# Hybrid trunk, layer 0's attention heads: later value products and joins, earlier raw weight loads, output weights on GpSimd's queue

## The chip, the cores and the metric

The kernel runs on one core of a Trainium2 chip. The time is device microseconds of one execution. Three executions before the change took 2606.33, 2608.89 and 2603.97 us (median 2606.33); a fourth was profiled.

A core has five instruction streams. PE is TensorE (its weight loads are told apart as PEld), DVE is VectorE, ACT is ScalarE, POOL is GpSimd and SP is SyncE. Each works through its own list in order and stops where an instruction waits for another engine or a transfer. Transfers are issued by SP's list or by POOL's, on two different queues, and are carried by the same 16 DMA engines.

## The reference

One sequence of 1024 rows of width 1024 goes through two layers: a token mixer, a residual add and a squared-ReLU MLP each. Layer 0's mixer is what the change touches:

```python
def dilated_attention(h, w_in, w_out):
    qkv = (h @ w_in).reshape(B, S, N_GROUPS, 3, ATTN_HEADS, HEAD_DIM)
    cos, sin = rope_tables(S, HEAD_DIM)
    for g, (window, dil) in enumerate(((128, 1), (512, 4), (2048, 16))):
        q = apply_rope(qkv[:, :, g, 0], cos, sin) * (HEAD_DIM ** -0.5)
        k = apply_rope(qkv[:, :, g, 1], cos, sin)
        v = qkv[:, :, g, 2]
        o_g, lse_g = dilated_group_attention(q, k, v, dil, window // dil)
        ...
    alpha = jax.nn.softmax(jnp.stack(lses, axis=0), axis=0)
    o = jnp.sum(alpha[..., None] * jnp.stack(outs, axis=0), axis=0)
    return o.reshape(B, S, ATTN_WIDTH).astype(h.dtype) @ w_out
```

There are 8 heads of width 128, and each head attends in three groups (dilations 1, 4, 16). The three outputs of a head are merged with weights from their softmax denominators. Everything is float32; the kernel multiplies matrices as three products of split operands (high by high, high by low, low by high).

## The kernel before

The values of all groups come first (lines with `pA` and `pB`). Then 24 steps follow, one per head and group: step p has head p // 3 and group p % 3. A step multiplies the normed input by the query and key weights of its group, in seven products of a Strassen-like scheme, in the order `SLOTS = (0, 1, 3, 2, 6, 4, 5)`. Each product is split in two halves of six matmuls (128x128 by 128x512). So a step has 14 half products, and these are its clock.

All other work of the heads is hung on this clock. `at(t, fn, rank)` puts a piece of work on an agenda, and `advance()`, which is called behind every half product, runs what is due, in the order of the ranks. With c = 14 p for the step that runs, the pieces are:

- `column` (L1121 to L1145), four times a step at c+5, c+11, c+13, c+15: DVE adds two products into a half of q or k (L1127), SP swaps its halves by two transfers (L1128 and L1129, `cw<-c`), and four half products later DVE turns it with the rotary tables and writes `qT` or `kT` (L1136, L1137 and L1139 or L1144). The last of these, half of `qT`, falls on c+5 of the next step.
- `follow`: the attention of the step before. It has four pairs of row blocks. `scores` (PE, L989) at c+8, c+8, c+12, c+12, then `soft` (DVE L1003, ACT L1005), then `halves` at c+11, c+12, c+15, c+16 (ACT L1035 splits the weights into 16-bit halves, POOL writes them to `pscr`, L1037), then `flip` at c+14, c+15, c+18, c+19 (SP reads them back transposed, L1048, `pt<-pscr`), then `values` at c+20, c+20, c+24, c+24 (PE multiplies them by v, L1069, `pO`; behind the second and the fourth pair ACT copies the result and SP stores it into `og`). c+20 is c+6 of the step behind. The last two steps' attention uses transposes on PE instead.
- `load`: the raw weights of the step behind, four transfers of 256 KB (L1119). `stage` splits them on ACT (L536) and DVE (L537).
- `plan_merges`: when a head's three groups are done, in the steps of group 1 and after. For each half of the rows SP loads 780 KB of `rows` (L1207), DVE makes the weights (`merge_weights` L1214 and L1215, `merge_shares` L1220 to L1223), ACT scales (L1227) and DVE joins (`merge_join` L1231 and L1232); SP stores the join into `oscr`.

```python
POINTS = (8, 8, 12, 12), (11, 12, 15, 16), (20, 20, 24, 24), (14, 15, 18, 19)   # scores, halves, values, flips
...
for s in self.SLOTS:
    for half in range(2):
        self.product(p, s, range(2 * half, 2 * half + 2))
        advance()
```

In the last step (p = 23) the output projection's first weights are fetched as well: `W.dma` (L136, 512 KB each) twice at c+1 and twice at c+2, at rank 0, and at c+3 `ahead_h8` (L1292), which loads 1 MB of joined heads (`ol`). `turned.turn` transposes `ol` on PE at c+8 (L260).

Tiles named k4 share 25 buffers and t2 tiles share 8; a tile takes over a buffer when what used it is done, and the instruction that first writes it waits for that. There are eight PSUM banks. A transfer also waits until the transfer issued eight places before it on its list has landed.

Of the kernel before, what the change touches and what calls it, by code (L numbers as in the profile page):

```python
# [20 lines left out]
P = 128  # L21
# [21 lines left out]
def hybrid_trunk(ctx, tc, x, norm_mix, norm_mlp, norm_fin, a_in, a_out, g_in, g_up, g_b, g_nw,  # L43
                 g_out, m_up, m_down, tab, msk, gmask, ident_d, out):
    nc = tc.nc
    pe, act, dve, pool, sp = nc.tensor, nc.scalar, nc.vector, nc.gpsimd, nc.sync
# [7 lines left out]
    def h8(shape, dt, name):  # L54
        return wk.tile(shape, dt, name=name, tag="h8", bufs=12)

    def k4(shape, dt, name):
        return wk.tile(shape, dt, name=name, tag="k4", bufs=25)

    def t2(shape, dt, name):  # L60
        return wk.tile(shape, dt, name=name, tag="t2", bufs=8)
# [50 lines left out]
    class Weights:  # L112
# [14 lines left out]
            self.slots.append(src)  # L127
            self.by.append(by)

        def dma(self):  # L130
            n = self.ndma
            if n < len(self.slots):
                self.ndma += 1
                src = self.slots[n]
                self.raws[n] = k4([P] + list(src.shape[1:]), F32, "raw")
                sp.dma_start(self.raws[n], src)  # L136

        def prep(self, eng=dve):
            n = self.nprep
# [41 lines left out]
    W = Weights()  # L181
# [104 lines left out]
    class Split:  # L286
# [4 lines left out]
        @staticmethod  # L291
        def at(tiles, k):
            n = 4 // len(tiles)
            return tiles[k // n][:, k % n, :]
# [442 lines left out]
    oscr = drp.tile([S, D], F32, name="oscr")  # L737
# [241 lines left out]
    class Attention:  # L979
# [104 lines left out]
        def plan(self, c, points, turn, values, flip=None):  # L1084
            self.by_dma = flip is not None

            def get():
                self.v = load_values(self.g, self.h)
            at(c + points[0] - 2, get)
            for j in range(4):  # L1090
                t = c + points[j]
                at(t, lambda j=j: self.scores(j), 2)
                at(t + 1 + (j % 2 and points[j] == points[j - 1]), lambda j=j: self.soft(j), 2)
                if self.by_dma:
                    at(c + turn[j], lambda j=j: self.halves(j), 3)
                    at(c + flip[j], lambda j=j: self.flip(j), 3)
                else:
                    at(c + turn[j], lambda j=j: self.turn(j), 3)
                at(c + values[j], lambda j=j: self.values(j), 4)

    class Heads(Up):
# [54 lines left out]
        def plan(self, p):  # L1156
            c = 14 * p
            st = self.st.setdefault(p, {})
            self.behind = True

            def keep(b, name):
                def fn():
                    e = t2([P, 512], F32, name)
                    act.activation(e, st[b], AF.Copy)
                    st[name] = e
                return fn
            at(c + 3, keep("X", "e1"), 0)
            at(c + 5, lambda: self.column(p, 0, 0, st["Y"], st["e1"]), 1)
            at(c + 7, keep("V", "e5"), 0)
            at(c + 9, keep("X", "e2"), 0)  # L1170
            at(c + 11, lambda: self.column(p, 1, 0, st["V"], st["e2"]), 1)
            at(c + 13, keep("X", "e3"), 0)
            at(c + 13, lambda: self.column(p, 1, 1, st["X"], st["e5"]), 1)
            at(c + 15, lambda: self.column(p, 0, 1, st["Z"], st["e3"]), 1)
            if p == 0:
                for s, t in ((4, 1), (6, 3), (5, 5)):
                    at(c + t, lambda s=s: self.stage(p, s), 7)
            at(c + 3, lambda: self.load(p + 1))
            for s, t in ((0, 8), (1, 9), (2, 10), (3, 11), (4, 14), (6, 15), (5, 17)):
                at(c + t, lambda s=s: self.stage(p + 1, s), 7)  # L1180

        def run_head(self, p):
            self.plan(p)
            if p:
                self.follow(p - 1, 14 * p, self.POINTS if p < self.count - 1 else self.SINGLE)
            for s in self.SLOTS:
# [1 line left out]
                    self.product(p, s, range(2 * half, 2 * half + 2))  # L1188
                    advance()

        POINTS = (8, 8, 12, 12), (11, 12, 15, 16), (20, 20, 24, 24), (14, 15, 18, 19)
        SINGLE = (8, 10, 12, 14), (12, 14, 16, 18), (14, 16, 18, 20)

        def follow(self, p, c, points):
# [8 lines left out]
    def merge_load(h, half):  # L1203

        rows = (h8([P, 4, NG, HD + 2], F32, "rows") if h == HEADS - 1 and half else
                r6([P, 4, NG, HD + 2], "rows"))
        sp.dma_start(rows, og[h][512 * half:512 * half + 512].rearrange("(t p) g c -> p t g c", p=P))  # L1207
        return rows
# [71 lines left out]
    def merged(h, half, o):  # L1280
        if h < HEADS - 1:
            sp.dma_start(oscr[512 * half:512 * half + 512, HD * h:HD * h + HD].rearrange("(b p) c -> p b c", p=P), o)
        else:
            def last():
                t_head(h, half, o)
                reached.add((0, half))
            at(clock[0] + 7, last)

    def ahead_h8(pairs):

        t = h8([P, 4, 512], F32, "ol")
        sp.dma_start(t, oscr[512 * pairs:512 * pairs + 512, 0:512].rearrange("(b p) c -> p b c", p=P))  # L1292
        return [t[:, 0:2, :], t[:, 2:4, :]]

    def ahead_k4(p):
# [4 lines left out]
    def plan_merges(h, c):  # L1300

        rows, part = {}, {}

        def load(half):
            rows[half] = merge_load(h, half)

        def weigh(half):
            part[half] = merge_weights(rows[half])

        def join(half):  # L1310
            del part[half]
            merged(h, half, merge_join(rows.pop(half), dve))
        for half in range(2):
            t = c + 13 + 11 * half
            at(t, lambda half=half: load(half))
            if half and h == HEADS - 2:
                t += 9
            at(t + 4, lambda half=half: weigh(half), 9)
            at(t + 5, lambda half=half: merge_shares(rows[half], *part[half]), 9)
            for n in range(4):  # L1320
                at(t + 6 + n, lambda half=half, n=n: merge_scale(rows[half], part[half][1], n), 9)
            at(t + 10, lambda half=half: join(half), 9)
# [429 lines left out]
    ol = []  # L1752
    turned = Turned(ol, x[0])
    for p in range(heads.count):
        h, g = divmod(p, NG)
        if g == 1 and h:
            plan_merges(h - 1, 14 * p)
        if p == heads.count - 1:
            for k in range(0, KT, 2):
                add_rows(a_out, k)  # L1760
            c = 14 * p
            at(c + 1, lambda: (W.dma(), W.dma()), 0)
            at(c + 2, lambda: (W.dma(), W.dma()), 0)
            at(c + 3, lambda: ol.extend(ahead_h8(0)), 0)
            for t in (5, 6, 7, 8):
                at(c + t, lambda: W.prep(dve), 7)
            at(c + 8, lambda: turned.turn(0), 7)
            at(c + 9, lambda: (turned.load_x(0), turned.load_x(1)))
            at(c + 11, lambda: turned.turn(1), 7)
            at(c + 17, lambda: ol.extend(ahead_h8(1)), 9)  # L1770
        heads.run_head(p)
# [619 lines left out]
    ol, turn1 = [], []  # L2391
# [81 lines left out]
```

## Time and profile before

| | us |
|---|---|
| median of three executions | 2606.33 |
| the profiled execution | 2608.73 |
| its span | 2607.0 |
| PE busy | 2569.7 (99%) |
| DVE busy | 1865.2 (72%) |
| ACT busy | 1309.1 (50%) |
| granted TensorE clock, mean | 0.996 |

The span runs from the first to the last instruction that the profile shows; the profiled execution took 1.7 us more. PE's idle time is the difference of its busy time and the span, 37 us. The views of waits name, for each instruction that found its engine idle, what ended the wait. In rows of the timeline the first number is the start in us from the span's start, the second the duration, and a bracket gives the idle time ahead and what ended it.

The 24 steps with their attention lie between about 265 and 890 us.

### The profile page before, as it was taken

The page shows a single profiled execution, that of the slowest core. Times are in us where ns is not written, and L with a number is a line of the kernel's source. Part 1 is how long each engine was busy: PE and PEld are TensorE (multiplying, and loading weights), DVE is VectorE, ACT ScalarE, POOL GpSimd, SP SyncE. Part 2 cuts the span into 40 slices and gives each one's busy share as a digit, 9 for nine tenths or more (in the row PEclk, how much of TensorE's full clock was granted, in tenths as well). Part 3 has the DMA queues.
Part 4 walks back from the last instruction along what each step waited for, and adds up shares of the span by engine and source line. Part 5 has one row for each costly group of instructions (what it writes and reads, how often), then busy time and mean ns, then how long its engine had stood idle before and what let it go on. Part 6 is the DMA issues. An engine that isn't in the chain of part 4 may idle for free.

```text
span 2607.0 us, 33382 instructions
## 1 busy us (share of the span) xinstructions
PE 2569.7 (99%) x11901; PEld 2138.2 (82%) x11901; DVE 1865.2 (72%) x3018; ACT 1309.1 (50%) x2388; POOL 79.3 (3%) x132
## 2 busy tenths in 40 slices
PE   9999999999998999999999999999999999999998
PEld 7888888888787888888888888888888888888887
DVE  7745888888887668766657487887658866656567
ACT  6423566666665446555534345654426555553334
POOL 0000111111110000000000000000000000000000
PEclk9999999999999999999999999999999999999999
DMA  5543688788888732544775453463513544396543
GB/s 182 172 143 109 171 210 213 203 208 216 207 212 219 238 121 100 191 153 154 257 268 185 145 184 106 124 213 99 183 67 127 170 150 161 126 354 205 182 149 131
DMA packets 403705, 456.73 MB, mean 175 GB/s; under 512 B 92337, under 2 KB 264753, under 8 KB 403538
## 3 DMA queue, kind: packets, MB, share of 16 engines
q1 hardware_dynamic: 397250, 437.29, 55.3%
q0 software_dynamic: 6144, 17.05, 2.1%
q8 instruction: 93, 1.52, 0.2%
q14 instruction: 74, 0.61, 0.1%
q10 hardware_dynamic: 144, 0.26, 0.0%
HBM read 279.19 MB, written 133.10 MB: 158 GB/s over the span
## 4 chain that ended last, share of the span: by engine, by line
PE 87%; DMA 5%; DVE 4%; ACT 2%; SPq 1%; issue 1%; DVEq 0%; ACTq 0%
PE pX L599 15%; PE pB L1936 13%; PE pA L1936 10%; PE pV L599 9%; PE pB L830 8%; PE pA L830 5%; PE pY L599 5%; PE pZ L599 5%; PE pd L216 3%; PE pd L214 3%; PE pd L215 3%; DMA cw<-c 2%; DMA pt<-pscr 1%; PE pS L989 1%; PE pO L1069 1%
## 5 line engine op out<-in xcount | busy, mean ns | idle before, releaser
L1936 PE MATMUL pB<-dh 128*128 128x512 f32 x512 | 199.4, 389 | 0.0
L1936 PE MATMUL pB<-dh,dl 128*128 128x512 f32 x512 | 199.2, 389 | 0.0
L1936 PE MATMUL pB<-dl,dh 128*128 128x512 f32 x512 | 199.2, 389 | 0.0
L223 DVE TENSOR_TENSOR dl<-sin,dh 128x1024 fp32r<-128x1024 f32 x112 | 136.7, 1220 | 42.1 <-ACT dh L220 41.4
L220 ACT ACTIVATE dh<-sin 128x1024 fp32r<-128x1024 f32 x112 | 117.9, 1052 | 88.6 <-PE pB L1936 34.1
L220 ACT ACTIVATE dh<-kept 128x1024 fp32r<-128x1024 f32 x64 | 67.9, 1061 | 183.4 <-DVE kept L1901 138.1
L599 PE MATMUL pV<-s4h,wd 128*128 128x512 f32 x448 | 150.9, 399 | 0.0
L1936 PE MATMUL pA<-dh 128*128 128x512 f32 x384 | 149.4, 389 | 0.0
L1936 PE MATMUL pA<-dl,dh 128*128 128x512 f32 x384 | 149.4, 389 | 0.0
L1936 PE MATMUL pA<-dh,dl 128*128 128x512 f32 x384 | 149.4, 389 | 0.0
L1005 ACT ACTIVATE pt<-pt,orow 128x128 f32<-128x128 f32 (+1 forms) x192 | 84.7, 442 | 123.7 <-DVE orow L1003 122.5
L1936 PEld LDWEIGHTS pB<-dh 128*128 128x128 f32 x512 | 96.1, 188 | 20.0
L1936 PEld LDWEIGHTS pB<-dh,dl 128*128 128x128 f32 x512 | 96.1, 188 | 19.9
L1936 PEld LDWEIGHTS pB<-dl,dh 128*128 128x128 f32 x512 | 96.1, 188 | 19.9
L537 DVE TENSOR_TENSOR wal<-raw,wah 128x512 fp32r<-128x512 f32 x112 | 76.2, 686 | 41.1 <-ACT wah L536 41.1
L1069 PE MATMUL pO<-v,pt 128*128 128x128 f32 x560 | 79.2, 284 | 23.1 <-DMA pt<-pscr 22.7
L537 DVE TENSOR_TENSOR wbl<-t,wbh 128x1024 fp32r<-128x1024 f32 x56 | 68.6, 1225 | 46.3 <-ACT wbh L536 46.2
L608 ACT ACTIVATE c<-c 128x512 f32<-128x512 f32 x64 | 40.4, 631 | 118.6 <-DVE c L636 77.6
L1037 POOL DMA_DIRECT2D pscr<-pt x124 | 77.0, 621 | 752.3 <-ACT pt L1035 742.0
L1069 PEld LDWEIGHTS pO<-v,pt 128*128 128x128 f32 x560 | 73.5, 195 | 31.3 <-DMA pt<-pscr 27.7
L599 PEld LDWEIGHTS pV<-s4h,wd 128*128 128x128 f32 x448 | 84.2, 188 | 17.8 <-DVE rb L624 0.3
L223 DVE TENSOR_TENSOR dl<-kept,dh 128x1024 fp32r<-128x1024 f32 x64 | 78.4, 1225 | 24.7 <-ACT dh L220 18.7
(398 smaller groups left out, 7444.3 us busy)
## 6 DMA issues: line engine op xcount, KB each, us to landing
sin<-acts SPq DMA_DIRECT2D x112, 512.0 KB, 3.9
raw<-in_mlp_w_up_dram SPq DMA_DIRECT2D x64, 512.0 KB, 6.2
acts<-s SPq DMA_DIRECT2D x64, 512.0 KB, 3.3
raw<-in_mlp_w_down_dram SPq DMA_DIRECT2D x64, 512.0 KB, 4.7
raw<-in_attn_w_in_dram SPq DMA_DIRECT2D x98, 256.0 KB, 4.5
cw<-c SPq DMA_DIRECT2D x192, 128.0 KB, 3.2
acts<-c SPq DMA_DIRECT2D x64, 256.0 KB, 2.1
kept<-in_mlp_w_down_dram SPq DMA_DIRECT2D x32, 512.0 KB, 5.2
```

Of the source, the lines that this page charges most:

```text
L214: pe.matmul(ps, sh, mh, start=start, stop=False)
L215: pe.matmul(ps, sh, ml, start=False, stop=False)
L216: pe.matmul(ps, sl, mh, start=False, stop=stop)
L220: act.activation(hi, src, AF.Copy)
L223: dve.tensor_tensor(lo, src, hi.bitcast(F32), op=OP.subtract)
L537: self.remain(lambda: dve.tensor_tensor(lo, src, hi.bitcast(F32), op=OP.subtract))
L599: pe.matmul(st[b], u[:, k, :], v, start=first and k + n == 0, stop=k == 3 and n == 2, skip_group_check=True)
L830: pe.matmul(self.acc[s][t], a[:, c], b[:, k, :], start=fresh and m + k + v == 0, stop=m == 1 and k == 1 and v == 2, skip_group_check=True)
L1005: act.activation(pt[:, i, :128 * n], pt[:, i, :128 * n], AF.Exp, scale=-1.0, bias=m, accum_out=self.row[:, r, HD:HD + 1])
L1037: pool.dma_start(scr[512 * P * b:][:256 * P * nb * m].rearrange("(i p c) -> p i c", i=nb, p=P), part.rearrange("p (i c) -> p i c", i=nb))
L1069: pe.matmul(po[:, 2 * (j % 2) + i, :], self.turned(j, tile_, i, s), self.v[:, k0 // 128 + s, :], start=(s == 0), stop=(s == nk - 1))
L1936: pe.matmul(self.acc[s][t], a[:, k, c], b[:, k, :], start=fresh and m + k + v == 0, stop=m == 7 and k == 1 and v == 2, skip_group_check=True)
```

## The change

The raw weights' `load` moves from c+3 to c+1. The value products move from c+20 and c+24 to c+21 and c+25. All of `plan_merges` moves one half product later: the load of the rows from c+13 and c+24 to c+14 and c+25, weights, shares, scaling and joins with it (of head 6's second half only the load moves; the work behind it stays where it was). In the last step `W.dma` and the first `ahead_h8` are issued by POOL instead of SP.

```diff
-        def dma(self):
+        def dma(self, by=None):
...
-                sp.dma_start(self.raws[n], src)
+                (by or sp).dma_start(self.raws[n], src)
...
-            at(c + 3, lambda: self.load(p + 1))
+            at(c + 1, lambda: self.load(p + 1))
...
-        POINTS = (8, 8, 12, 12), (11, 12, 15, 16), (20, 20, 24, 24), (14, 15, 18, 19)
+        POINTS = (8, 8, 12, 12), (11, 12, 15, 16), (21, 21, 25, 25), (14, 15, 18, 19)
...
-    def ahead_h8(pairs):
+    def ahead_h8(pairs, by=sp):
...
-        sp.dma_start(t, oscr[512 * pairs:512 * pairs + 512, 0:512].rearrange("(b p) c -> p b c", p=P))
+        by.dma_start(t, oscr[512 * pairs:512 * pairs + 512, 0:512].rearrange("(b p) c -> p b c", p=P))
...
         for half in range(2):
-            t = c + 13 + 11 * half
+            t = c + 14 + 11 * half
             at(t, lambda half=half: load(half))
             if half and h == HEADS - 2:
-                t += 9
+                t += 8
             at(t + 4, lambda half=half: weigh(half), 9)
             at(t + 5, lambda half=half: merge_shares(rows[half], *part[half]), 9)
             for n in range(4):
                 at(t + 6 + n, lambda half=half, n=n: merge_scale(rows[half], part[half][1], n), 9)
             at(t + 10, lambda half=half: join(half), 9)
...
-            at(c + 1, lambda: (W.dma(), W.dma()), 0)
-            at(c + 2, lambda: (W.dma(), W.dma()), 0)
-            at(c + 3, lambda: ol.extend(ahead_h8(0)), 0)
+            at(c + 1, lambda: (W.dma(pool), W.dma(pool)), 0)
+            at(c + 2, lambda: (W.dma(pool), W.dma(pool)), 0)
+            at(c + 3, lambda: ol.extend(ahead_h8(0, pool)), 0)
```

On PE the first pair's and second pair's value products (`pO`) stand behind the first half of the product `pX<-s2`, where before they stood ahead of it:

```order
+L599 MATMUL pX<-s2l,wbh 128x512
+L599 MATMUL pX<-s2h,wbl 128x512
 L1069 MATMUL pO<-v,pt 128x128 x7
-L599 MATMUL pX<-s2h,wbh 128x512
-L599 MATMUL pX<-s2l,wbh 128x512
```

Six matmuls pass the products at c+6, and six others (`pX<-s3`) in the same way at c+10.

On SP, in the step of group 1, this is the stretch from the end of one step's stores to the next step's first flips (`og_70` is head 0's output, `rows` the merge's load):

```order
-L1207 DMA rows<-og_70 128x4x390
+L1082 DMA og_70<-orow 128x4x130
+L1128 DMA cw<-c 64x512
+L1129 DMA cw<-c 64x512
 L1048 DMA_TRANSPOSE pt<-pscr_96 128x1x256
 L1048 DMA_TRANSPOSE pt<-pscr_96 128x2x256
+L1207 DMA rows<-og_70 128x4x390
 L1128 DMA cw<-c 64x512
 L1129 DMA cw<-c 64x512
```

The load of the rows goes behind the first pair's flips, and the last store of `og` behind a pair of swaps. The four loads of raw weights (L1119) are in no such piece: they stand behind the second pair's flips and ahead of the third's in both kernels. They take other k4 buffers.

On DVE, in the step of group 2, the last rotary work on `qT` (L1136, L1137, L1144) passes the shares of the merge (L1220 to L1223):

```order
+L1127 TENSOR_TENSOR c<-pY,e_3043 128x512
+L1136 TENSOR_TENSOR cw<-cw,tab 128x512
+L1137 TENSOR_TENSOR c<-c,tab 128x512
+L1144 TENSOR_TENSOR qT<-c,cw 128x4x128
 L1220 TENSOR_TENSOR md<-me,rows 128x12
 L1221 TENSOR_REDUCE mz<-md 128x4
 L1222 RECIPROCAL mz<-mz 128x4
 L1223 TENSOR_TENSOR me<-me,mz 128x12
-L1127 TENSOR_TENSOR c<-pY,e_3037 128x512
```

POOL's list in the last step, where only writes of weights' halves stood:

```order
 L1037 DMA pscr_97<-pt 128x2x512
+L136 DMA raw<-in_attn_w_out_dram 128x1024 x2
 L1037 DMA pscr_98<-pt 128x2x512
+L136 DMA raw<-in_attn_w_out_dram 128x1024 x2
 L1037 DMA pscr_99<-pt 128x2x512
+L1292 DMA ol<-oscr 128x4x512
```

The third pair's write (`pscr_98`) now stands behind two weight loads and the fourth's (`pscr_99`) behind four.

## The prediction

> **What bounds the kernel now.** I read the page's first part, then PE's waits, then the timelines of PE, DVE and SP around the longest of them.
>
> ```profile
> PE 2569.7 (99%) x11901; PEld 2138.2 (82%) x11901; DVE 1865.2 (72%) x3018; ACT 1309.1 (50%) x2388; POOL 79.3 (3%) x132
> ...
> PE pO L1069 <- DMA pt<-pscr: 22.7, 19, 7.2
> PE pS L989 <- DVE qT L1144: 3.3, 3, 2.1
> ```
>
> PE is the bound; only its idle time, 37 us of the span, can go. The waits name 22.7 us of it before the value products, for the transposed read of the softmax weights (in total, 19 times, the longest 7.2), and 3.3 us before the scores, for the turned `qT`. No other wait of PE inside the heads is named. One of the 19 is in the last step; the other 18 hold 15.5 us:
>
> ```profile
>   PE pO L1069: 15.5, 18
> ```
>
> PE's waits asked over each group-2 attention's first value products and the scores that follow them (six answers, at 393, 470, 548, 624, 704 and 780 us), then three group-1 waits from the timeline:
>
> ```profile
> PE pO L1069 <- DMA pt<-pscr: 1.8, 2, 1.0
> ...
> PE pO L1069 <- DMA pt<-pscr: 1.1, 2, 0.7
> ...
> PE pS L989 <- DVE qT L1144: 1.0, 1, 1.0
> PE pO L1069 <- DMA pt<-pscr: 0.4, 1, 0.4
> ...
> PE pO L1069 <- DMA pt<-pscr: 1.5, 2, 0.8
> PE pS L989 <- DVE qT L1144: 0.2, 1, 0.2
> ...
> PE pO L1069 <- DMA pt<-pscr: 1.0, 1, 1.0
> ...
> PE pO L1069 <- DMA pt<-pscr: 2.5, 3, 1.1
> ...
> 523.96 1.16 PE L1069 MATMUL pO<-v,pt 128*128 128x128 f32 x8 [0.97 <-DMA pt<-pscr]
> 678.17 1.16 PE L1069 MATMUL pO<-v,pt 128*128 128x128 f32 x8 [1.70 <-DMA pt<-pscr]
> 756.03 1.16 PE L1069 MATMUL pO<-v,pt 128*128 128x128 f32 x8 [2.08 <-DMA pt<-pscr]
> ```
>
> That is 8.3 us in group 2, 4.75 in group 1, and 15.5 - 8.3 - 4.75 = 2.4 left, in the products at c+10. But the scores stand right behind these products, and their `qT` is barely in time (DVE's last rotary row, then PE's scores, in three steps):
>
> ```profile
> 475.39 1.17 DVE L1144 TENSOR_TENSOR qT<-c,cw 128x512 f32<-128x512 f32 x1
> 476.62 1.16 PE L989 MATMUL pS<-kT,qT 128*128 128x128 f32 x8
> ...
> 399.54 1.13 DVE L1144 TENSOR_TENSOR qT<-c,cw 128x512 f32<-128x512 f32 x1
> 401.80 1.05 PE L989 MATMUL pS<-kT,qT 128*128 128x128 f32 x8
> ...
> 756.38 1.10 DVE L1144 TENSOR_TENSOR qT<-c,cw 128x512 f32<-128x512 f32 x1
> 759.80 1.47 PE L989 MATMUL pS<-kT,qT 128*128 128x128 f32 x8
> ```
>
> At 476.56 the turn ends and at 476.62 PE uses it: no slack. At 401.80 there are 1.13 us, at 759.80 2.32. So a wait that goes from the value products can come back eight matmuls later, as a wait for DVE.
>
> **The change, part by part.** *The earlier load of raw weights* costs and brings nothing by itself. SP's order around it does not change, and SP was not held by a clock but by its list:
>
> ```profile
> 388.88 2.48 SPq L1048 DMA_TRANSPOSE pt<-pscr  x2
> ...
> 392.76 2.57 SPq L1048 DMA_TRANSPOSE pt<-pscr  x2
> 395.42 2.18 SPq L1119 DMA_DIRECT2D raw<-in_attn_w_in_dram  x4
> ```
>
> The loads follow the flips without a pause, as they will after the change. What is left is other buffers; I count 0.
>
> *The later value products.* A half product is worth 6 starts at full clock: below, 845.76 - 844.40 = 1.36 us. Every wait at L1069 can shrink by this if the flips land when they do now.
>
> Group 1: 0.97 + 1.36 + 1.36 = 3.7 us, and `qT` has room: 2.32 us in the longest case, and the four share instructions go behind it. The rows' load now stands between the first and second pair's flips, but it was ahead of both; what the second flip waits for stays the same. I take 3.7, bounds 0 and 4.75.
>
> Group 2: by the flips alone 1.36 in three steps and all of the others. By `qT`, only what DVE gains. DVE's waits in the same stretches, the first step and the fourth:
>
> ```profile
> DVE cw L1136 <- DMA cw<-c: 0.9, 1, 0.9
> DVE mz L1214 <- DMA rows<-og: 0.6, 1, 0.6
> ...
> DVE cw L1136 <- DMA cw<-c: 0.6, 1, 0.6
> ```
>
> Both stand ahead of the last turn. The merge's weights (`mz`) move behind the next column's sum, so that DVE no longer stops for the rows there, and the pair of swaps that queued behind the 780 KB of rows now goes ahead of them. That frees 0.6 to 1.5 us a step; I take 1.0 in the four steps without slack (the second to the fifth), where 1.0 to 1.5 us could go, and 1.36 in the first and sixth: 6.7. Bounds: 1.1 (only the shown slack of the first step) and 8.3 + 1.2.
>
> The 2.4 us at c+10: all four are below 1.36 on average, but the next step's `qT` decides again. I take 1.5, bounds 0 and 2.4.
>
> *The last step.* PE's longest wait and what follows, and SP's list ahead of it:
>
> ```profile
> 840.45 2.08 PE L1069 MATMUL pO<-v,pt 128*128 128x128 f32 x8 [7.24 <-DMA pt<-pscr]
> 842.18 0.77 PE L599 MATMUL pX<-s2h,wbh 128*128 128x512 f32 x1
> ...
> 844.40 0.39 PE L599 MATMUL pX<-s2h,wbl 128*128 128x512 f32 x1
> ...
> 845.76 0.39 PE L599 MATMUL pX<-s2h,wbl 128*128 128x512 f32 x1
> 845.99 0.82 PE L989 MATMUL pS<-kT,qT 128*128 128x128 f32 x4
> 846.64 1.04 PE L260 MATMUL pT<-ident,ol 128*128 128x128 f32 x8
> ...
> 828.89 1.06 SPq L136 DMA_DIRECT2D raw<-in_attn_w_out_dram  x2
> 830.05 0.48 SPq L1128 DMA_DIRECT2D cw<-c  x1
> ...
> 831.35 3.98 SPq L1048 DMA_TRANSPOSE pt<-pscr  x1
> ```
>
> The second pair's flip, at 831.35, queues behind 1 MB of output weights. The wait also slows PE: the eight products took 2.08 us against 1.16 above, and the next five starts 2.22 us against 5 x 0.227, together 2.0. So 9.2 us can go at most. After the change the rows stand there instead of the weights. In step 20 a flip behind rows and swaps was issued at 749.64 and its products started at 756.03, 6.4 us later; 831.35 + 6.4 = 837.7, where the products are due at 833.2 + 1.36 = 834.6. So 3.1 us of wait stay and the scores come 6 us sooner. What is late next is `ol`: its 1 MB landed 9.2 us after its issue at 836.51 and PE transposes it at 846.64. On POOL it can be issued once the fourth pair's write is, 829.81 plus four issues of 0.7, about 832.5, so it lands at 841.7 by the same 9.2 us; PE would be there at about 840.5. The gain is then 846.64 - 841.7 = 5 us. Against this stand the writes of the third and fourth pair, which POOL now queues behind 1 and 2 MB. I take 4, bounds -2 and 9.2.
>
> One row speaks against this move, the fourth pair's write before the change (its issue at 829.8 on POOL, then its landing, beside all earlier ones):
>
> ```profile
> DMA to landing us min/median/max: 9.6/9.6/9.6
> ...
> DMA to landing us min/median/max: 1.8/3.4/6.6
> ```
>
> It was on POOL's own queue and waited all the same while SP's weights moved. The Trainium skill, "DMA: Bandwidth & Descriptors", section "Issuing engines are not separate DMA queues", says that transfers issued by any engine run on the same 16 DMA engines and interleave, so that another issuer saves only issue time. By that rule the 7.24 us shrink only by the 1.36 of the later products, and the sum below would be 2.6 us less; the row agrees with the rule.
>
> **Sum:** 3.7 + 6.7 + 1.5 + 4 = 15.9 us. Against the profiled execution's 2608.73 that is 2592.8; this execution lies 2.4 above the median of the three, against which it would be 2590.4. I forecast 2592.
>
> **The rivals.**
>
> 1. *DVE takes the wait's place.* The flips come in time, but the scores wait for `qT` wherever it has no slack. For: the rows at 476; two waits of this kind stand in the answers above. Against: DVE has idle time ahead of the turn. Group 1 keeps 3.7, group 2 only 1.1 and what the sixth step's slack gives (0.6), c+10 nothing, the last step 1.5: 7 us, about 2600.
> 2. *The bytes, not the queue, set the last step.* The last step gives 1.4 instead of 4: about 2595.
> 3. *No change.* The flips are late because the DMA engines are busy (0.85 from 295 to 830 us, first row below), so the reads fall behind by as much as the products are put off. Against: the flips are tied to the softmax, which is not moved. About 2606.
> 4. *Slower: the rows come too late.* A half's load now waits on SP for the first pair's flips, 2.5 us (the 388.88 row), or for the store of the later products; the weights that need it come only 1.36 later and still stand ahead of the last turn. For: DVE waits for rows already in the first group-2 step (0.6 us above). Against: the swaps ahead of them are short. It decides once the rows land over 1.36 us later than now. If they land 4 us later, the six group-2 steps lose their 6.7 us and pay 2.6 us each on top, 15.6: 15.6 - 3.7 - 1.5 - 4 = 6.4 us slower, about 2615.
>
> ```profile
> 295.00:830.00 535.00, 517.83 (x2584) 436.93 (x2584) 448.24 (x954) 326.10 (x840) 73.04 (x119) 1.00 0.85 208
> 830.00:872.00 42.00, 32.63 (x178) 27.95 (x177) 31.28 (x58) 20.02 (x49) 0.52 (x1) 0.91 1.02 265
> ```
>
> (Columns: stretch, length, busy PE, PEld, DVE, ACT, POOL, granted clock, DMA share, GB/s.) The second row is the last step: DMA is full, and the clock was 0.91, against 1.00.
>
> **How the numbers follow.** Forecast 0.44, rival 1 0.21, rival 2 0.11, rival 3 0.13, rival 4 0.11. Forecast and rivals 1 and 2 are faster by over 0.2% (5.2 us, about what a measurement of this kernel tells from no change): 0.76. The same 0.13, slower 0.11. With all upper bounds, and 5 us in the last step, the gain is 4.75 + 9.5 + 2.4 + 5 = 21.7 us, 2584.7 against the median. Upward the forecast passes into rival 1 at 2600, and 2607 takes in rivals 1 and 2 and the greater part of rival 3. I give 2584 to 2607.
>
> **What would show it.** PE's wait at L1069 for `pt<-pscr` should fall from 22.7 us to 3 to 6, with at most one over 2 us, at about 835 us; the wait at L989 for `qT` should not pass 5 us in all (10 would be rival 1). DVE's waits for `rows<-og` should be gone; 10 us of them, with waits at L989 behind them, would be rival 4. SP's four loads L1119 should stand where they stood. In the last step a wait of PE for `ol` of 0 to 3 us at L260 is expected; the granted clock there should be over 0.91. The sum is wrong if PE's idle time falls by less than 8 us.

## The result, and the profile after

The changed kernel takes 2624.22 us (median of four, 2623.31 to 2624.43), the kernel before 2607.59 beside it: a ratio of 1.0062, 95% interval 1.0048 to 1.0076. It is some 16 us slower, where I forecast 15.9 us faster (2592). The profiled execution's span is 2622.7 us and PE's busy time 2570.7, so PE's idle time rose from 37.3 to 52.0 us.

PE's waits in the heads, as the list of the whole execution has them (in total, times, longest):

```profile
PE pO L1069 <- DMA pt<-pscr: 20.9, 11, 6.8
PE pX L599 <- ACT e L1164: 11.0, 11, 3.6
PE pS L989 <- DVE qT L1144: 9.6, 6, 2.4
```

The first and third answer to 22.7 and 3.3 us before; the second is new. Together 41.5 us against 26.0: the difference, 15.5 us, is about the whole loss. The wait for the flips hardly shrank, the one for `qT` grew and one for ACT's copies came beside it. Waits of DVE and ACT that feed them:

```profile
DVE c L1127 <- DMA og<-orow: 18.4, 13, 2.3
DVE mz L1214 <- DMA rows<-og: 13.5, 11, 5.2
ACT me L1216 <- DVE md L1215: 68.8, 15, 9.9
```

Before, the first had no row among DVE's waits, the second had 3.6 us and the third 26.6. How the third reaches PE, in one step (ACT's list, then PE's):

```profile
395.28 0.21 ACT L1216 ACTIVATE me<-md 128x12 f32<-128x12 f32 x1 [4.95 <-DVE md L1215]
...
396.22 0.58 ACT L1164 ACTIVATE e<-pX 128x512 f32<-128x512 f32 x1
...
396.85 0.50 PE L599 MATMUL pX<-s2h,wbh 128*128 128x512 f32 x1 [1.54 <-ACT e L1164]
```

The copy that frees `pX` stands behind the merge's exponent on ACT's list and ends at 396.80; PE, which has waited for it, starts at 396.85. The stretches that the prediction showed, now:

```profile
295.00:830.00 535.00, 503.74 (x2509) 422.48 (x2508) 436.04 (x925) 316.80 (x819) 70.32 (x114) 0.99 0.86 203
830.00:872.00 42.00, 33.73 (x168) 28.52 (x167) 31.17 (x58) 22.43 (x51) 6.28 (x10) 0.92 0.89 234
```

PE is busy for 14 us less in the first stretch (503.74 against 517.83). The last step's first matmul starts at 840.26 against 824.22, 16.0 us later, so the loss is made in the steps ahead of the last one.

"Group 1" and "group 2" here and in the prediction name the step in whose plan the work stands. Its products at c+20 run at c+6 of the step behind and belong to the attention of the group before: what the prediction calls group-2 attention is attention of group 1.

The longest new wait before the value products shows where a forecast term went. SP's list and PE's in a step of group 1, after the change:

```profile
602.11 0.54 SPq L1207 DMA_DIRECT2D rows<-og  x1
...
603.99 3.53 SPq L1048 DMA_TRANSPOSE pt<-pscr  x1
...
612.84 2.07 PE L1069 MATMUL pO<-v,pt 128*128 128x128 f32 x8 [4.75 <-DMA pt<-pscr]
614.57 0.77 PE L599 MATMUL pX<-s2h,wbh 128*128 128x512 f32 x1
```

The same place before:

```profile
590.36 0.54 SPq L1207 DMA_DIRECT2D rows<-og  x1
591.00 2.50 SPq L1048 DMA_TRANSPOSE pt<-pscr  x2
...
594.88 1.77 SPq L1048 DMA_TRANSPOSE pt<-pscr  x1
```

The second pair's flip now follows the 780 KB of rows by 1.9 us (603.99 - 602.11); before, by 4.5 us. The issues of these two flips and their time to landing, after and then before:

```profile
pt<-pscr SPq DMA_TRANSPOSE x1, 8.8
```

```profile
pt<-pscr SPq DMA_TRANSPOSE x1, 4.6
```

So this flip takes 4.2 us longer to land. It is also issued 2.0 us later against PE's own work (6.25 us behind the first matmul of the step at 597.74; before, 4.25 us behind the one at 590.63). PE, which comes to the products about 1.5 us later, waits 4.75 us. It then also runs slower: eight products in 2.07 us, as in the prediction's last step (2.08), against 1.16 after the shorter waits of the rows in the prediction.

This is the longest of six. In the other such steps whose landing the trace has, the flip lands after 6.3 to 7.1 us, before after 4.5 to 6.4, and its issue is 0.7 us earlier to 1.0 us later. In all seven runs that load the rows one half product later (the change, e2 to e4, e8, e9 and e13) the flip needs 6.4 to 8.8 us where the rows went out 1.8 to 1.9 us ahead of it. In the kernel before and the other runs they went out 4.3 us or more ahead, and it needs 3.5 to 6.9 us.

### The profile page after: what moved, and what is told of

It reads as the page before. It is cut to its first block, busy times and chain, and to the rows that moved or that the text cites. A ratio compares the mean times of both kernels' runs of the same rounds, so it can differ in the third digit from the quotient of the medians.

```text
span 2622.7 us, 33363 instructions
## 1 busy us (share of the span) xinstructions
PE 2570.7 (98%) x11901; PEld 2136.0 (81%) x11901; DVE 1866.7 (71%) x3018; ACT 1309.5 (50%) x2388; POOL 82.3 (3%) x137
## 4 chain that ended last, share of the span: by engine, by line
PE 85%; DMA 5%; DVE 5%; ACT 2%; issue 1%; SPq 1%; DVEq 0%; ACTq 0%
PE pX L599 14%; PE pB L1936 13%; PE pA L1936 10%; PE pV L599 9%; PE pB L830 7%; PE pA L830 5%; PE pZ L599 5%; PE pY L599 4%; PE pd L216 3%; PE pd L214 3%; PE pd L215 3%; DMA cw<-c 2%; PE pS L989 2%; DMA rows<-og 1%; PE pO L1069 1%
## 5 line engine op out<-in xcount | busy, mean ns | idle before, releaser
L599 PE MATMUL pX<-s2h,wbh 128*128 128x512 f32 x224 | 91.2, 407 | 8.6 <-ACT e L1164 8.6
```

What stands on the lines that cost most here:

```text
L599: pe.matmul(st[b], u[:, k, :], v, start=first and k + n == 0, stop=k == 3 and n == 2, skip_group_check=True)
```

## The experiments

Each run was compared with the kernel before, executed beside it. The medians of that kernel were 2606.5 to 2608.9 us beside the experiments. Differences in us below are the ratio less one, times 2607, unless two medians are named. "A" is the merges' move, "B" the value products' move, "C" the raw weights' load, "D" the queue.

| run | parts or edit | median us | ratio, 95% interval |
|---|---|---|---|
| change | A B C D | 2624.22 | 1.0062 (1.0048 to 1.0076) |
| e1 | B C D | 2606.81 | 0.9991 (0.9982 to 1.0001) |
| e2 | A C D | 2617.73 | 1.0034 (1.0023 to 1.0044) |
| e3 | A B D | 2624.41 | 1.0061 (1.0046 to 1.0077) |
| e4 | A B C | 2622.65 | 1.0056 (1.0041 to 1.0071) |
| e5 | B | 2603.30 | 0.9984 (0.9974 to 0.9994) |
| e6 | B, first and second pair only | 2598.33 | 0.9970 (0.9960 to 0.9981) |
| e7 | B, third and fourth pair only | 2610.09 | 1.0015 (1.0006 to 1.0024) |
| e8 | A | 2615.71 | 1.0041 (1.0026 to 1.0056) |
| e9 | A, loads of rows only | 2632.10 | 1.0099 (1.0083 to 1.0116) |
| e10 | A, work only | 2608.46 | 1.0005 (0.9996 to 1.0015) |
| e11 | e6, second half's shares later | 2599.41 | 0.9971 (0.9958 to 0.9984) |
| e12 | D | 2613.00 | 1.0025 (1.0016 to 1.0034) |
| e13 | A, first half's load only | 2621.91 | 1.0058 (1.0035 to 1.0081) |
| e14 | e6 and A's work | 2607.85 | 1.0000 (0.9990 to 1.0009) |
| e15 | e6, merges one earlier | 2586.61 | 0.9917 (0.9903 to 0.9932) |
| e16 | merges one earlier | 2588.79 | 0.9917 (0.9902 to 0.9932) |
| e17 | B, merges one earlier | 2601.50 | 0.9973 (0.9963 to 0.9984) |

### Taking one part out of the change (e1 to e4)

Against the changed kernel, e1 has

```diff
-            t = c + 14 + 11 * half
+            t = c + 13 + 11 * half
...
-                t += 8
+                t += 9
```

> The change with its merges put back (rows' loads at c+13 and c+24 and the work behind them as before; later value products, earlier raw loads and POOL's queue stay). Theory M (the merge came one half product too late): in the changed kernel the load of the rows stands between the two pairs' flips and DVE's merge weights stand behind a column and a turn, ACT waits in order for them (68.8 us at L1216, 26.6 before) and its copies of pX are late. Then this kernel loses the 11.0 us of PE waits for ACT's copies (under 2 us left), ACT's wait at L1216 is near 27 us, DVE's wait for rows is under 5 us, and PE's pO waits fall from 20.9 to about 10. About 2605 us or less. Theory S (the later products store og later, and the store keeps a buffer and the rows back): DVE's wait of 18.4 us for og<-orow stays, the rows still land late, the waits for ACT's copies stay over 7 us, and the time is 2617 or more.

Measured: 2606.81, near the time of theory M, 18 us less than with A. PE's waits before the value products outside the last step are down to 2 us (11.9 less 9.0 and 0.7 there). But 8.6 us for ACT's copies and 8.8 for `qT` stay, as theory S had it. Both are in it: A makes the loss, and B alone trades one wait for others.

e2 puts the value products back, against the changed kernel:

```diff
-        POINTS = (8, 8, 12, 12), (11, 12, 15, 16), (21, 21, 25, 25), (14, 15, 18, 19)
+        POINTS = (8, 8, 12, 12), (11, 12, 15, 16), (20, 20, 24, 24), (14, 15, 18, 19)
```

> The change with its value products put back to c+20 and c+24. Theory S: DVE's waits for the store of og fall from 18.4 us to about 6 as before, the rows land earlier, the waits of PE for ACT's copies fall from 11.0 to under 4, and the time is about 2608. Theory M: the merge weights still stand behind column and turn, the waits for ACT's copies stay at 8 us or more, pO waits are 22 or more, and the time is 2620 or more.

2617.73 lies between the two theories, nearer to M's 2620. The waits for ACT's copies are gone altogether, and those for flips are 30.1 us: without B the late flips show at PE first. With A in place B costs 7 us (1.0062 against 1.0034).

e3 and e4 put back the load (c+3 for c+1) and SP's queue:

```diff
-            at(c + 1, lambda: self.load(p + 1))
+            at(c + 3, lambda: self.load(p + 1))
```

> The change with only the raw weights' load put back to c+3. SP's order is the same as in the changed kernel; only buffers differ. Theories M and S both expect 2624 within 2 us and PE's waits within 2 us each. A third theory L (the four k4 buffers taken earlier make other tiles wait) expects under 2619 with DVE's 18.4 us for og<-orow gone or the waits for ACT's copies down by 4 us.

2624.41 against 2624.22: the earlier load of raw weights does nothing, as the prediction counted.

```diff
-            at(c + 1, lambda: (W.dma(pool), W.dma(pool)), 0)
-            at(c + 2, lambda: (W.dma(pool), W.dma(pool)), 0)
-            at(c + 3, lambda: ol.extend(ahead_h8(0, pool)), 0)
+            at(c + 1, lambda: (W.dma(), W.dma()), 0)
+            at(c + 2, lambda: (W.dma(), W.dma()), 0)
+            at(c + 3, lambda: ol.extend(ahead_h8(0)), 0)
```

> The change with only the last step put back: output weights and first joined heads on SP's queue. Changes nothing before 818 us. If POOL's queue gains what the later products alone don't (my forecast's 4 us less 1.4), this is 2.6 us slower: 2627. If only the bytes count, it is 2624 within 1.5 us. If POOL's queue itself makes the last step late (the step's pO wait was 6.85 us and ol was issued 6.6 us late), it is faster: about 2620, with the scores of the last step but one at 885 us or earlier instead of 889.

1.6 us faster, with overlapping intervals: not resolved. The last step's flip wait fell from 6.85 to 3.70 us, but a wait for `qT` of 3.63 us follows it.

### The value products by themselves (e5 to e7)

e5 makes the POINTS edit alone, on the kernel before; e6 and e7 make half of it each:

```diff
-        POINTS = (8, 8, 12, 12), (11, 12, 15, 16), (20, 20, 24, 24), (14, 15, 18, 19)
+e5:     POINTS = (8, 8, 12, 12), (11, 12, 15, 16), (21, 21, 25, 25), (14, 15, 18, 19)
+e6:     POINTS = (8, 8, 12, 12), (11, 12, 15, 16), (21, 21, 24, 24), (14, 15, 18, 19)
+e7:     POINTS = (8, 8, 12, 12), (11, 12, 15, 16), (20, 20, 25, 25), (14, 15, 18, 19)
```

> The kernel before with only the later value products (c+21 and c+25). In the run with the merges put back PE's waits at c+6 were gone from the value products, but DVE's sum for the last column of q stood 1.8 us for the store of og, whose buffer it takes over, and PE then waited 8.6 us for ACT's copies and 8.8 us for qT. Theory S (this buffer): the same here, c<-og<-orow 12 us or more on DVE, pO waits outside the last step under 4 us, pX and qT waits together over 12 us; the last step has SP's queue again, so about 2605. Theory Q (no buffer: qT's chain is simply full, rival 1 of the prediction): the same time, but the waits for qT start where no store is waited for. What tells S and Q apart are the next two runs.

> Only the first and second pair's products later (c+21), the third and fourth stay at c+24, so the second store of og is issued ahead of the swaps of the column at c+11, as before, and the last column of q no longer takes over its buffer. Theory S: DVE's wait c<-og<-orow is near 0 to 5 us, the pX waits for ACT's copies are under 2 us, the pO waits at c+6 go as in the run before, and some of it comes back as qT waits of 3 to 5 us: about 2600, 5 us faster than with all products later. Theory Q: waits for qT of 8 us or more, and 2605 or more.

> Only the third and fourth pair's products later (c+25), the first two at c+20. Theory S: the column takes over the store's buffer again (DVE's wait c<-og<-orow over 10 us), and the waits at c+6 stay as before, since they are those of the first pairs; the turn of qT is late besides: slower than before by 3 to 8 us, 2612 to 2617. Theory Q: the pO waits at c+10 (2.4 us) go and nothing else changes: 2606 to 2608.

Measured: -4, -8 and +4 us. e5 and e6 came near theory S in time; e7, at 2610.09, lies between S (2612 to 2617) and Q (2606 to 2608). DVE's wait for the store, of e5, then of e6:

```profile
DVE c L1127 <- DMA og<-orow: 14.0, 16, 2.0
```

```profile
DVE c L1127 <- DMA og<-orow: 2.6, 4, 1.4
```

With the second store at c+11 it is issued behind the swaps of that half product's column, and the last column of `q` takes over the buffer that it still reads. Left at c+10 it is not. So the later products at c+10, which I put at 1.5 us of gain, cost 4 us. PE's waits in e6, though, speak against the rest of theory S:

```profile
PE pX L599 <- ACT e L1164: 7.7, 6, 2.6
PE pS L989 <- DVE qT L1144: 6.4, 6, 1.3
PE pO L1069 <- DMA pt<-pscr: 5.3, 6, 2.7
```

The waits for ACT's copies stay without the store's buffer. The flips are in time at c+6 (0.7 us of waits are left there of 13.2), and 14.1 us of other waits stand in their place. What e6 gains is elsewhere: the last step's flip wait is 2.69 us instead of 7.24, and PE's busy time 2566.4 instead of 2569.7.

### What PE waits for once the flips are in time (e11)

In e6 ACT's copy of `pX` stands behind the first scalings of the merge, which wait for DVE's shares. e11 puts it ahead of them, on top of e6:

```diff
-            at(t + 5, lambda half=half: merge_shares(rows[half], *part[half]), 9)
+            at(t + 5 + (half and h < HEADS - 2), lambda half=half: merge_shares(rows[half], *part[half]), 9)
...
-                at(t + 6 + n, lambda half=half, n=n: merge_scale(rows[half], part[half][1], n), 9)
-            at(t + 10, lambda half=half: join(half), 9)
+                at(t + 6 + n + (half and h < HEADS - 2), lambda half=half, n=n: merge_scale(rows[half], part[half][1], n), 9)
+            at(t + 10 + (half and h < HEADS - 2), lambda half=half: join(half), 9)
```

> The run with the first pairs later, plus one edit: in the second half of each merge (heads 0 to 5) shares, scaling and join one half product later, weights and load where they were. On ACT the copy of pX then stands ahead of the scaling, which waits 3 us in order for DVE's shares. Theory ACT (what is late at c+6 once the flips are in time is ACT's copy, behind the merge's scaling): PE's waits for ACT's copies fall from 7.7 to under 2 us, qT comes 0.7 us sooner because the shares stand behind the turn of kT's input, and the time is about 2592. Rival: qT's chain is as late as before and takes what the copies give back: waits for qT over 10 us, and within 2 us of 2598.

PE's waits in e11:

```profile
PE pS L989 <- DVE qT L1144: 12.2, 7, 3.0
PE pO L1069 <- DMA pt<-pscr: 6.9, 6, 3.1
PE pX L599 <- ACT e L1164: 1.5, 1, 1.5
```

My theory fell: the waits for ACT's copies went (7.7 to 1.5), and the waits for `qT` took all of it (6.4 to 12.2). No difference in time. With the merges in this place DVE's turn of `qT` is the next limit, which was rival 1 of the prediction.

### The merges by themselves (e8, e9, e10, e13)

On the kernel before, e8 makes A's edit (with `t += 8` for head 6), e9 moves only the loads, e13 only the first half's load, e10 only weights, shares and scaling:

```diff
-            t = c + 13 + 11 * half
+e8:         t = c + 14 + 11 * half
-            at(t, lambda half=half: load(half))
+e9:         at(t + 1, lambda half=half: load(half))
+e13:        at(t + (not half), lambda half=half: load(half))
-            at(t + 4, lambda half=half: weigh(half), 9)
-            at(t + 5, lambda half=half: merge_shares(rows[half], *part[half]), 9)
-                at(t + 6 + n, lambda half=half, n=n: merge_scale(rows[half], part[half][1], n), 9)
+e10:        at(t + 5, lambda half=half: weigh(half), 9)
+e10:        at(t + 6, lambda half=half: merge_shares(rows[half], *part[half]), 9)
+e10:            at(t + 7 + n, lambda half=half, n=n: merge_scale(rows[half], part[half][1], n), 9)
```

> The kernel before with only the merges one half product later. Theory M: this part costs by itself, about 10 us (2618), with pO waits at c+6 of group 1 behind the rows (5 us in all or more longer than before) and ACT's wait at L1216 over 45 us. If the loss needs the later products beside it (a rows' load behind the later store), it is within 3 us of the kernel before.

> The kernel before with only the load of the rows one half product later (c+14, c+25); weights, shares, scaling and joins stay. Theory F (flips): the loss of the merges' part comes from the 780 KB that now go out 2 us ahead of the second pair's flip in the step of group 1 (4.5 us before), which then lands 7 us after its issue instead of 4.6. Then this run has the same group-1 waits at c+6 as the run with the merges alone (16.7 us in six steps, 4.75 before) and takes 2612 to 2617. Theory G (the work: DVE's weights behind the column, ACT in order behind them): no more than 3 us slower than before; group-1 waits near 5 us.

> The kernel before with only the first half's load of the rows later (c+14), the one that goes between the flips in the step of group 1; the second half's load and all work of the merge stay. If the flips are the cost (theory F), nearly all of the 25.6 us of the run with both loads later is here: 2625 or more, with group-1 waits of 11 us or more at c+6. If the second half's load is half of it (DVE stops for rows ahead of the last turn in group 2), this is about 2618, and its group-2 waits are those of the kernel before (8.3 us).

> The kernel before with only the work of the merge one half product later (weights, shares, scaling; load and join stay). Theory F: 2605 to 2609, group-1 waits as before (about 5 us); DVE no longer waits for rows. Theory G: 2612 or more, ACT's wait at L1216 over 40 us.

A alone costs 11 us, its loads alone 26 (theory F had 2612 to 2617, 2632.10 was measured), the first half's load alone 15 (2621.91, between its two expectations), the work alone nothing that is resolved. So the place of the load decides, and what moves with it gives back part of it; the joins move only in e8, and no run has them alone. e9's waits of DVE and PE say why the 26 is more than theory F had:

```profile
DVE mz L1214 <- DMA rows<-og: 40.5, 14, 4.9
```

```profile
PE pO L1069 <- DMA pt<-pscr: 36.1, 17, 6.0
```

The weights stand where they stood and DVE stops 2.9 us on average for rows that come later. Theory F held for the group-1 flips (waits at c+6 of 13.2 us in e9, 16.3 in e13, 16.7 in e8, 4.75 before) but left out this second cost: the waits at c+6 of group 2 are 16.9 us in e9, 8.3 before.

The waits are not all of it. PE's named waits grow by 13.5 us in e9 (39.5 against 26.0), its span by 22.2. The rest is busy time, 2578.5 us against 2569.7 for the same 11901 matmuls, at a mean granted clock of 0.993 against 0.996.

### The queue by itself (e12)

D's edit alone, on the kernel before (the diff is that of the change's last step).

> The kernel before with only the output weights and the first joined heads on POOL's queue. Changed against the kernel without the queue, the last steps took 57.1 instead of 53.6 us, so POOL's queue costs 1 to 4 us there: 2608 to 2611, with the wait for pt<-pscr in the last step 7 to 9 us as before (7.24). If my forecast of the queue holds after all it is 2603 to 2605, with that wait under 4 us. Nothing before 818 us changes.

6.5 us slower, 2 us above the expected range. PE waits for flips in the last step, where it waited 7.24 us once:

```profile
PE pO L1069 <- DMA pt<-pscr: 10.1, 3, 5.1
```

POOL's list and then SP's in the last step of e12:

```profile
823.00 1.15 POOL L136 DMA_DIRECT2D raw<-in_attn_w_out_dram  x2
826.95 0.72 POOL L1037 DMA_DIRECT2D pscr<-pt  x1 [2.80 <-ACT pt L1035]
827.67 1.23 POOL L136 DMA_DIRECT2D raw<-in_attn_w_out_dram  x2
```

```profile
824.32 0.55 SPq L1207 DMA_DIRECT2D rows<-og  x1
824.97 2.95 SPq L1048 DMA_TRANSPOSE pt<-pscr  x2
```

The landings of the first pair's two flips (median), in e12 and in the kernel before:

```profile
pt<-pscr SPq DMA_TRANSPOSE x2, 12.7
```

```profile
pt<-pscr SPq DMA_TRANSPOSE x2, 3.8
```

On SP the weights were issued at 828.89, behind rows and flips. POOL's list has nothing ahead of them and issues them at 823.00, ahead of both, and the flips come 9 us later. The Trainium skill, "DMA: Bandwidth & Descriptors", section "Issuing engines are not separate DMA queues", says that transfers of any issuer interleave on the same engines and that another issuer saves only the time of issuing. The trace agrees that they interleave: weights on POOL's queue go with later landings on SP's. What it shows beside this is the sooner issue, by 5.9 us for the first megabyte; that this alone does the harm, and not also the third pair's write, which now lands after 9.8 us instead of 3.7, is argued and not shown.

### The merge's work with the products later (e14)

e6's POINTS and e10's edit together.

> First pairs' products later (as the run of 2598) and the merge's weights, shares and scaling one half product later; loads of rows and joins stay. My forecast's term (DVE no longer stops for the rows, qT 1.0 us sooner in each group-2 step): DVE's 3.8 us of waits for rows are gone, the waits for ACT's copies and qT (14.1 us together) fall by 4 to 6, about 2593. Rival (ACT waits in order for the later weights, its copy of pX stays late): the waits for ACT's copies stay at 7 us or more and the time is 2597 to 2602.

2607.85, worse than either theory: 8 us slower than e6. DVE's wait for rows is down to 1.3 us, so the stop is gone, as the prediction wanted it. But ACT's wait for the weights, in order ahead of its splits and copies, rose:

```profile
ACT me L1216 <- DVE md L1215: 52.0, 15, 5.8
```

It is 26.6 us in e6. DVE, rid of the rows, waits for swaps instead, 45.1 us where e6 has 34.0. That row of DVE's, and PE's waits:

```profile
DVE cw L1136 <- DMA cw<-c: 45.1, 30, 3.2
...
PE pS L989 <- DVE qT L1144: 10.0, 7, 3.1
PE pX L599 <- ACT e L1164: 8.6, 6, 2.5
PE pO L1069 <- DMA pt<-pscr: 7.5, 9, 3.3
```

The wait for `qT`, which was to fall, is 10.0 us against 6.4 in e6, and the one for ACT's copies 8.6 against 7.7. So my term for DVE has the wrong sign. Which of the two longer stops, ACT's for the weights or DVE's for the swaps, makes `qT` later is not shown; in e10 ACT's same wait is 50.3 us and nothing is lost that is resolved.

### The merges the other way (e15 to e17)

```diff
-            t = c + 13 + 11 * half
+            t = c + 12 + 11 * half
...
-                t += 9
+                t += 10
```

e16 is this alone, e15 with e6's POINTS, e17 with e5's.

> First pairs' products later and the whole merge one half product EARLIER (loads at c+12 and c+23, the work with them; head 6's second half keeps its work). If the rows' place decides, the load gets further ahead of the second pair's flip (one pair of swaps more between), the group-1 waits stay under 1 us and rows are there in time: 2594 to 2598. Rival: the store of og has not landed at c+12, SP stops for it with swaps and flips behind, and the weights stand ahead of the columns on DVE: 2600 or more.

> The kernel before with only the merges one half product earlier (loads c+12 and c+23, work with them). If the rows' place on SP decides by itself, this gains about as much as it lost when moved later (8.3 us): 2596 to 2601, DVE's waits for rows under 1 us, PE's c+6 waits in group 2 still there (6 to 9 us), since the first pairs' products are not later. If the gain needs the later products (qT then free to use), it is 2602 or more.

> All four pairs' products later (c+21, c+25) and the merges one half product earlier. If the second store of og behind the swaps of c+11 and its buffer cost what they cost before (5 us between the runs of 2603 and 2598), this is 2590 to 2593 with DVE's wait c<-og<-orow over 10 us. If that wait was only a cost because the merge's weights were late too, it is within 2 us of 2587.

e16 is 20 us faster than the kernel before by its median, e15 is at 2586.61: with either, both kernels of this study are beaten, and between the two nothing is resolved. Both missed their expectations, which ended at 2596 and 2594, on the good side. PE's waits in e16:

```profile
PE pO L1069 <- DMA pt<-pscr: 11.1, 10, 3.7
PE pS L989 <- DVE qT L1144: 1.2, 3, 0.7
```

I had expected that the waits at c+6 of group 2 stay, since the products are not later. They went, from 8.3 us to 0.1. The last step's wait is 3.74 us instead of 7.24, and PE's busy time 2564.9 us instead of 2569.7. The waits at c+6 of group 1 did not go: 5.1 us before the second pairs' products, against 4.75. The place in group 2 in the timeline of the kernel before (SP, then POOL):

```profile
611.74 0.36 SPq L1076 DMA_DIRECT2D og<-orow  x1
612.16 0.50 SPq L1207 DMA_DIRECT2D rows<-og  x1
...
612.42 1.19 POOL L1037 DMA_DIRECT2D pscr<-pt  x2 [17.64 <-ACT pt L1035]
```

and of e16:

```profile
602.54 0.45 SPq L1207 DMA_DIRECT2D rows<-og  x1
606.93 0.36 SPq L1076 DMA_DIRECT2D og<-orow  x1
...
607.61 1.19 POOL L1037 DMA_DIRECT2D pscr<-pt  x2 [18.94 <-ACT pt L1035]
```

The first of these writes and its time to landing in us, before and then in e16:

```profile
pscr<-pt POOLq DMA_DIRECT2D x1, 64.0 KB, 6.4
```

```profile
pscr<-pt POOLq DMA_DIRECT2D x1, 64.0 KB, 3.8
```

Before, the 780 KB stand behind a store of `og` on SP and go out 0.3 us ahead of the first write of softmax weights, which the flip needs; the write takes 6.4 us. One half product earlier in the plan the rows pass that store and go out 5.1 us ahead of the write, which takes 3.8. The first writes of the six such steps took 6.1, 6.4, 3.0, 6.4, 5.9 and 6.2 us before, and 4.3, 3.7, 3.7, 3.8, 2.8 and 3.2 in e16; they are also issued 0.8 to 2.2 us earlier against PE's work. Load and work move together here, so what the load does by itself in this direction was not tried. In group 1 the second pair's flip follows the rows by 8.2 us:

```profile
581.73 0.36 SPq L1207 DMA_DIRECT2D rows<-og  x1
...
589.97 1.23 SPq L1048 DMA_TRANSPOSE pt<-pscr  x1
```

There this flip lands after 5.5 us, no sooner than after the 4.5 us before (4.6): a longer lead gains nothing more.

e17 missed its expectation by 9 us. Its list in the same step:

```profile
585.44 0.53 SPq L1082 DMA_DIRECT2D og<-orow  x1
589.16 0.37 SPq L1207 DMA_DIRECT2D rows<-og  x1
...
590.83 2.84 SPq L1048 DMA_TRANSPOSE pt<-pscr  x2
...
595.07 1.31 SPq L1048 DMA_TRANSPOSE pt<-pscr  x1
```

With all products later the store goes behind the swaps of c+11, and the load, which reads what it writes, is issued 3.7 us behind it with nothing between. The flips stand behind this load: the second pair's is issued 7.4 us behind the first matmul of its step (587.68), in e15 4.2 us, and PE's waits at c+6 of group 1 are 8.2 us in e17 and none in e15. DVE's waits for rows are 9.0 us in e17 and 0.5 in e15, those for the store's buffer 9.8 and 4.6. So the held list accounts for some 8 of the 15 us between the two; the rest is not taken apart.

## Why the prediction was wrong

**Group 1, 3.7 us of gain.** The step that failed is "what the second flip waits for stays the same". It looked at which semaphore the flip waits for, not at what lies ahead of it on the DMA engines. In the step shown the rows came from 4.5 to 1.9 us ahead of the flip and its landing went from 4.6 to 8.8 us; over all six the waits rose from 4.75 to 11.8 us (0.57, 2.55, 0.99, 4.75, 1.20 and 1.71 in the list of PE's rows after). e13, with that load alone, takes 15 us more and has 16.3 us of these waits. The mirrored e16 has 5.1: bringing the load nearer costs, taking it further off gains nothing here.

**Group 2, 6.7 us of gain.** The 1.36 us by the flips came: 2.3 us of 8.3 are left before the value products at c+6. What failed is "that frees 0.6 to 1.5 us a step" on DVE. DVE's stop for the rows did not go but grew, 3.6 to 13.5 us, since the rows are issued later and take longer (7.1 to 9.1 us to land in these steps, 6.0 to 6.8 before). And where it does go (e14), DVE stops for swaps and ACT for the later weights, and `qT` is later, not sooner. I looked at the queue behind the waiting DVE instruction and not at ACT's, where the splits of the softmax weights and the copies that free `pX` stand behind the merge's exponent; in the changed kernel that costs PE 11.0 us. Rival 1 was right in mechanism: in e6 and e11 the waits for `qT` and for the copies take what the flips give at c+6, even without A.

**c+10, 1.5 us of gain.** Wrong sign. The store behind the later products passes a pair of swaps on SP, which the order rows in the part on the change show, and holds a t2 buffer for the last column: e5 less e6, 4 us of cost.

**The last step, 4 us of gain.** Wrong sign: 6.5 us of cost alone (e12), in the full change not resolved (e4). The step "on POOL it can be issued once the fourth pair's write is" was about `ol`; that the 2 MB ahead of it would go out 5.9 and 7.8 us sooner than on SP, the first of them ahead of rows and flips, was not asked. With the products later and the weights left on SP's queue, 3.75 us of the wait of 7.24 are left in e5, 2.69 in e6 and 3.70 in e4: about the forecast's 4 us go without the queue that was to bring them. What brings them is open, since e16, whose products are not later, has 3.74. The bytes rival was right about the engines and still too kind.

**The raw weights' load, 0.** Right, with the other parts in place (e3).

**Rival 3's reason** that the flips are tied to the softmax, which is not moved, is not enough by e16: between the two stands the write of the softmax weights, and in five of six steps it takes 1.8 to 3.1 us less to land when the rows go out earlier.

**Rival 4** is what happened, with its signs (13.5 us of waits for rows, 9.6 us at L989 behind them), at a chance of 0.11 and priced at 6.4 us slower where 16 were measured. It counted only the group-2 steps; the group-1 flips and ACT's 68.8 us were not in it.

By the parts alone, A +10.7, B -4.2 and D +6.5, with C at 0 by e3, make +13.0; the change measures +16.2. The remaining 3 us are less than the intervals of the four add up to.

## What to carry to other kernels

When a large transfer is moved by one place, ask what is issued in the next few microseconds behind it, on every queue, and who waits for that: here the merges, with their loads of 780 KB, moved by one half product (1.36 us) either way were worth +11 or -20 us, beside the 22.7 us of waits that the change was aimed at. A late small transfer can be late because of a large one ahead of it; try the large one earlier before putting off the reader. And when work moves on one engine, look also at the engine that waits for it in order: its other work moves too.

## What the runs showed of the hardware

- A transposing read of this kernel needs 3.5 to 6.9 us to land when 780 KB were issued 4.3 to 8.2 us ahead of it, and 6.4 to 8.8 us when they were issued 1.8 to 1.9 us ahead; with 1 MB of weights and the rows ahead, two such reads took 12.7 us against 3.8 (e12).
- A 64 KB write on POOL's queue took 6.4 us with 780 KB issued 0.3 us ahead on SP's queue, and 3.8 us with them 5.1 us ahead; five of six such steps show the like. So a load on one queue goes with later landings on the other.
- Putting DMA issues on an idle list is not neutral: that list does not hold them back, so they pass transfers that they stood behind (823.00 against 828.89 us in e12).
- A wait of PE cost more than its length: after stops of 4.5 us and more before these products the next eight, where the trace has all of them, took 2.07 to 2.08 us instead of 1.16, and over the whole program PE's busy time moved with the waits (2578.5 us in e9, 2569.7 before, 2564.9 in e16, for the same matmuls).
